# Turning x by 32-bit words on TensorE, each word behind a 512-column matmul, with five block pairs in place of ten

## The chip, the core and the metric

The kernel runs on one core of a Trainium2 chip. A core has five engines that work from queues of their own and wait for each other through counters (semaphores): TensorE (PE in the profile; its weight loads are PEld), VectorE (DVE), ScalarE (ACT), GpSimd (POOL) and SyncE (SP, which here only issues transfers). The metric is the device time of one execution in microseconds. The profile is of one execution; its span is the stretch from its first to its last recorded event.

## What is computed

```python
y = np.matmul(x, weight)                       # x: 16 x 512 x 768, weight: 768 x 768, float32
y = y.reshape(batch, seq, n_heads, head_dim)   # 12 heads of 64
y1, y2 = y[..., :32], y[..., 32:]
out1 = y1 * cos1 - y2 * sin1                   # cos, sin: 512 x 64, halves 1 and 2
out2 = y2 * cos2 + y1 * sin2
out = np.concatenate([out1, out2], axis=-1)    # float32
```

It is a projection of 8192 rows followed by a rotation of each head's two halves.

## The kernel before, in words

The 8192 rows are 64 tiles of 128 rows; four tiles make a group (QB = 4, groups g = 0 to 15). A tile's 768 input columns are six chunks of 128 (CHUNKS: three t, two e). Weights are cast to fp16 once (`w_sb`).

**A tile's way.** SP loads x into one of NX = 10 buffers `xs` (`load`, L210). ACT casts it to fp16 into one of five buffers `xc` (`cast`, L245); the cast orders the columns so that for each t the two values of e lie side by side. TensorE turns it so that input columns lie on partitions (`turn`, L256, or `turn_rows`, L271), into the PSUM pair `pt`. One copy on ACT (L190, the line of the helper that makes all copies) brings it to one of eight buffers `xt`. TensorE multiplies (L337 at both ends of the program, L362 for groups 1 to 14) into six PSUM banks `py`. DVE multiplies the banks by cos and sin (L419, products in `tq` or in the memory of `w_raw`), POOL adds the two halves of the products (L445), and ACT or SP issues the stores (L477).

**Two halves.** From group 1 on each matmul uses one half of the array, rows 0 to 63 (r = 0) or 64 to 127 (r = 1). `walk` (L344) writes each half's list: of every 1536 output columns, banks 0 and 2 in matmuls of 512 columns, bank 1 in matmuls of 256, six chunks each. The second half starts 1024 columns later in the lists (LAG) and takes the banks in another order, so that both halves don't write one bank at once. `both` (L375) merges the two lists by the columns issued so far (`at`). `turn_rows` writes twelve transposes between two calls of `both`: six chunks times two halves, in turn, 64 columns each, the halves into pt0 and pt1. Its copy reads both.

**Blocks.** Ten pairs of tiles (`BLOCKS`, L140: the second half of groups 5 to 13 and of the last) aren't turned by TensorE. Their x is loaded by quarters in such an order (`load_quarter`, L225) that DVE's 32 x 32 stream transpose (`turn_pair`, L299) does the turning: it moves 32-bit words of two fp16 values. Six pairs are loaded by SP as fp32 and cast by ACT (`cast_pair`); four are loaded by POOL, which casts on the way.

**The order.** It is written out in Python: in the main loop (L668 on) each step calls `both` three times, and between these `turns`, `bturns`, `casts`, `pool_loads` and the stores that are due. `do` (L42) adds the waits: an instruction waits for the writers of what it reads and for the readers of what it overwrites; TensorE doesn't wait for itself unless `after` says so. `pump` (L517) issues loads as buffers come free. An fp32 identity (`ident32`) is made by POOL at group 2 in a part of `w_raw`, for an addition at the very end (`add_pe`, L451).

Of the kernel before, what the change touches and what calls it, by code (L numbers as in the profile page):

```python
# [10 lines left out]
FP32 = mybir.dt.float32  # L11
FP16 = mybir.dt.float16
# [4 lines left out]
class Flow:  # L17
# [24 lines left out]
    def do(self, e, make, reads=(), writes=(), dma=None, tick=True, after=0):  # L42
        need = {}
        for k in reads:
            for s, v in self.wrote.get(k, {}).items():
                need[s] = max(need.get(s, 0), v)
        for k in writes:
            for d in (self.wrote, self.readby):
                for s, v in d.get(k, {}).items():
                    need[s] = max(need.get(s, 0), v)  # L50
        if e == "pe":
            need.pop("pe", None)
            if after:
                need["pe"] = after
        waits = self.settle(e, need)
        for s, v in waits[:-1]:
            self.eng[e].wait_ge(self.sem(s), v)  # L57
        i = make(self.eng[e])
        if waits:
            s, v = waits[-1]  # L60
            i.wait_op(self.sem(s), v, "sem-ge")
        name, step = (dma, 16) if dma else (e, 1)
        self.sem(name)
        self.order[name] = len(self.order) + sum(self.count.values())
        at = self.count[name] + step
        if tick or dma:
            i.then_inc(self.sems[name], step)
            self.count[name] = at
            self.known[name, at] = dict(self.seen[e])
        for k in reads:  # L70
            d = self.readby.setdefault(k, {})
            d[name] = max(d.get(name, 0), at)
        for k in writes:
            self.wrote[k] = {name: at}
            self.readby[k] = {}
        return i
# [32 lines left out]
def kernel(  # L109
# [11 lines left out]
    f = Flow(nc, tc)  # L121
    do = f.do
    P = nc.NUM_PARTITIONS

    B, S, H = x.shape
# [5 lines left out]
    NT = H // (2 * P)  # L131
    SB = S // P
    QB = 4
    NG = B * SB // QB
    NTILE = QB * NG
    CHUNKS = [(t, e) for t in range(NT) for e in range(2)]
# [1 line left out]


    BLOCKS = {}  # L140
    for g in range(5, 14):
        BLOCKS[g, 1] = "pool" if g % 2 == 0 and g >= 4 else "sp"
    BLOCKS[LAST, 1] = "sp"

    def sbuf(name, shape, dt):
        return nc.alloc_sbuf_tensor(name, shape, dt).ap()

    NX, NB, NBH, NC, NCP, NXT, NXP, NOV = 10, 3, 3, 5, 2, 8, 4, 4

    ident = sbuf("ident", [P, P], FP16)  # L150
    cold = sbuf("cold", [P, 512], FP16)
    sin_sb = sbuf("sin_sb", [P, SB, D], FP32)
    csn = sbuf("csn", [P, 2, SB, D], FP32)
# [18 lines left out]
        v = mem[:, base : base + 2 * n].rearrange("p (j n) -> p j n", j=2)  # L172
        return v[:, :, lo:hi], sorted(keys)

    ident32 = w_flat[:, 3072 : 3072 + P]
    HOMES0, HOMES, HOMESL = (0, 1024, 3072, 4096), (6144, 0, 3072), (0, 1024, 2048, 3072, 4096, 5120)
    ov_b = [sbuf(f"ov{i}", [P, QB * H], FP32) for i in range(NOV)]
    py = nc.alloc_psum_tensor("py", [P, 6 * 512], FP32).ap()
# [1 line left out]
    pt_b = [pt2[:, i] for i in range(2)]  # L180
# [7 lines left out]
    def copy(e, o, i_):  # L188
        return lambda eng: (
            eng.copy(out=o, in_=i_) if e == "act" else eng.tensor_copy(out=o, in_=i_)  # L190
        )
# [57 lines left out]
    def turn(i, e):  # L249
# [8 lines left out]
        do(e, copy(e, xt_b[z], pt), reads=[f"pt{k}"], writes=[f"xt{z}"])  # L258
        xT[i] = (lambda t, h: xt_b[z][:, t, h, :], f"xt{z}")

    def turn_rows(i, e):

        c = xc[i]
        z = ring("xt", NXT)
        src = xc_b[c].rearrange("p (t m e) -> p t e m", t=NT, e=2)
        pts = [pt_b[r].bitcast(FP16)[:, 0 : H // 2].rearrange(
            "p (t e m) -> p t e m", t=NT, e=2) for r in range(2)]
        for t, h in CHUNKS:
            for r in range(2):
                rows = ts(r, HP)  # L270
                do("pe", lambda eng: eng.transpose(  # L271
                    pts[r][:, t, h, :], src[rows, t, h, :], ident[rows, rows]),
                    reads=[f"xc{c}", "ident"], writes=[f"pt{r}"], tick=(t, h) == CHUNKS[-1])
        do(e, copy(e, xt_b[z].rearrange("p t e (r m) -> p r (t e) m", r=2),
                   pt2.bitcast(FP16)[:, :, 0 : H // 2].rearrange("p r (c m) -> p r c m", m=HP)),
           reads=["pt0", "pt1"], writes=[f"xt{z}"])
        xT[i] = (lambda t, h: xt_b[z][:, t, h, :], f"xt{z}")

    def cast_pair(gh, e="act"):
        k = xs[gh]  # L280
# [40 lines left out]
    def pieces(g, s):  # L321

        out_, lo = [], s * H
        for c0, c1, ps, banks, _ in units(g):
            step = 512 if len(banks) > 1 else c1 - c0
            for k, b in enumerate(banks):
                a, z = max(lo, c0 + k * step), min(lo + H, c0 + (k + 1) * step)
                if a < z:
                    out_.append((a, z, ps[:, a - c0 : z - c0], b))
        return out_  # L330
# [27 lines left out]
    def one(g, i, a, z, r, c, opens, start, ends, whole):  # L358
        s, rows, (t, h), bank = i % QB, ts(r, HP), c, a // 512
        get, key = xT[i]  # L360
        after = closed[g, bank] if not opens and c == CHUNKS[0] else 0
        do("pe", lambda eng: eng.matmul(  # L362
            py[:, a:z], get(t, h)[rows], w_sb[rows, t, h, a - s * H : z - s * H],
            start=start, stop=not opens and ends and whole, skip_group_check=True),
            reads=[key, f"w{t}{h}"], writes=[f"ps{bank}"], tick=ends, after=after)
        if ends and whole and opens:
            closed[g, bank] = f.count["pe"]
        if ends and whole and not opens:
            ready.setdefault(g, set()).add(bank)
# [5 lines left out]
    def both(upto):  # L375

        while True:
            n = [(at[r], r) for r in (0, 1) if lines[r]]
            if not n or min(n)[0] >= upto:
                return  # L380
            r = min(n)[1]
            cols, what = lines[r].pop(0)
            at[r] += cols
            one(*what)
            g = what[0]
            for u in units(g):
                k = g, u[0]
                if k not in roped and {b for b in range(u[0] // 512, u[1] // 512)} <= ready.get(g, set()):
                    roped.add(k)
                    rope(g, u)  # L390
# [76 lines left out]
    def store(g, c0, c1, e):  # L467
# [16 lines left out]
    do("pool", lambda eng: eng.affine_select(  # L484
        out=ident, in_=ident, compare_op=mybir.AluOpType.not_equal, fill=1.0,
        base=0, pattern=[[-1, P]], channel_multiplier=1), writes=["ident"])

    order = [0, 1, "w0", 2, "w1", "w2", 3, "w3", "w4", "w5"]
    for k in order:
# [98 lines left out]
    assert not quarters  # L588
    pump()

    rows_on = [False]
    state = {"cast": 4, "turn": 4, "bturn": 0, "pool": 0}
    pairs = sorted(BLOCKS)
# [14 lines left out]
    def turns(upto, most=NTILE):  # L608
        while state["turn"] < min(upto, NTILE) and most > 0:
            i = state["turn"]  # L610
            state["turn"] += 1
            if not is_block(i):
                most -= 1
                (turn_rows if rows_on[0] else turn)(i, "act")

    def bturns(upto):
        while state["bturn"] < len(pairs):
# [50 lines left out]
    for i in range(QB, NTILE):  # L668
        g, s = divmod(i, QB)
        us = units(g)  # L670
        done_to = (s + 1) * H
        rows_on[0] = QB <= i <= QB * LAST
        if i == QB * (LAST - 2) + 2:
            cast_pair((LAST, 1))
            xb_used[0] += 1
        if i < ROWS:
            if s % 2 == 0:
                for r in range(2):
                    lines[r].extend(walk(i // 2, r))
            for n in range(1, 4):  # L680
                both((i - QB) * 4608 + n * 1536)
                if n == (1 if i > QB else 2):
                    turns(i + T_AHEAD, 1)
        if i == ROWS:
            both(NTILE * 4608)
        for n, p in enumerate(pieces(g, s)) if i >= ROWS else ():
            a, z, _, bank = p
            if n == 1 and i < QB * LAST:
                turns(i + T_AHEAD, 1)
            for c in CHUNKS:  # L690
                mm_piece(i, p, c, c == CHUNKS[0], c == CHUNKS[-1],
                         tick=c == CHUNKS[-1])
            for u in us:
                if u[1] == z:
                    rope(g, u)
        bturns(i + (B_AHEAD if i < QB * (LAST - 2) else 9))
        if i == 2 * QB:
            do("pool", lambda eng: eng.tensor_copy(out=ident32, in_=ident),
               reads=["ident"], writes=["ident32", "wr20"])
        turns(i + 1 + (T_AHEAD if i > QB else 2), 1)  # L700
        casts(i + 1 + (C_AHEAD if i > QB else 4), 1 + i % 2)
        pool_loads(i + P_AHEAD)
        for q in stores.get(i, ()):
            store(*q)
        if g == LAST:
            if s == 2:
                store(g, 0, H, "sp")
            if s == 3:
                store(g, H, 2 * H, "act")
# [44 lines left out]
```

## Time and profile before

| | us |
|---|---|
| median of 3 runs (lowest to highest) | 150.45 (150.42 to 150.75) |
| span of the profiled execution | 148.2 (148.15 unrounded) |
| TensorE busy in it | 140.8 |
| DVE busy | 126.0 |
| POOL busy | 121.8 |
| ACT busy | 79.0 |

The time of a run is some 2.3 us above the profiled span, for what lies around it. The profile's rows of groups give an engine, an operation, its tiles and shapes, the count, the busy time, the mean duration in ns, and the idle time before it with its releaser. A matmul's record lasts longer than its hold on the array, since matmuls are pipelined; how close they follow each other is read from the starts. In the chain and in the timelines a row gives its start and its length.

### The profile page before, as it was taken

To read this page: it belongs to the slowest core of one execution; us is meant where nothing else is said; L and a number is where in the kernel's file an instruction comes from. 1 tells how busy PE (TensorE), PEld (TensorE's weight loads), DVE (VectorE), ACT (ScalarE), POOL (GpSimd) and SP (SyncE) were. 2 spreads that over 40 slices of the span, in tenths; PEclk is the share of its full clock that TensorE was granted. 3 is DMA by queue.
4 is the path that set the end of the run, shared out by engine and by line. 5 is a ranking of instruction groups with operands and counts; after the bars stand their busy time and mean duration, and the time that the engine had idled before them with its cause. 6 is when DMAs were issued, how large, how long until landed. Compare 5 with 4: busy or idle time off the path is not lost.

```text
span 148.2 us, 4422 instructions
## 1 busy us (share of the span) xinstructions
PE 140.8 (95%) x1948; PEld 112.7 (76%) x1948; DVE 126.0 (85%) x99; ACT 79.0 (53%) x94; POOL 121.8 (82%) x73
## 2 busy tenths in 40 slices
PE   6789999999999999999999999999999999999980
PEld 2335578888888888888888888888888888765860
DVE  0335998886988899899989998999989999999991
ACT  3453898777777933557261915375263919931010
POOL 1000396999999998999999999879699999999990
PEclk9999999999999999999999999999999999999999
DMA  3999999999999999999999999999999999998675
GB/s 124 352 395 403 402 406 398 373 379 296 317 366 330 352 353 277 294 408 287 319 355 397 379 323 358 365 408 324 381 365 337 411 409 416 410 408 333 264 297 180
DMA packets 27555, 51.67 MB, mean 349 GB/s; under 512 B 6160, under 2 KB 13072, under 8 KB 27536
## 3 DMA queue, kind: packets, MB, share of 16 engines
q1 hardware_dynamic: 15824, 28.84, 57.0%
q10 hardware_dynamic: 7360, 20.97, 35.9%
q0 software_dynamic: 4352, 1.57, 8.6%
q8 instruction: 15, 0.25, 0.7%
q14 instruction: 4, 0.03, 0.1%
HBM read 27.79 MB, written 25.17 MB: 357 GB/s over the span
## 4 chain that ended last, share of the span: by engine, by line
PE 78%; DVE 12%; DMA 4%; issue 1%; SPq 1%; DVEq 0%
PE py L362 68%; DVE tq L419 8%; PE py L337 5%; PE pt L271 4%; DMA w_raw<-in_weight_dram 4%; DVE w_raw L419 2%; SPq L210 1%; PE pt L256 1%; DVE ov L445 1%; DVE xs L419 1%; SPq L232 1%; DVE w_sb L190 0%; DVEq L57 0%; SPq L749 0%; SPq L119 0%
## 5 line engine op out<-in xcount | busy, mean ns | idle before, releaser
L445 POOL TENSOR_TENSOR ov<-tq 128x512 f32<-128x512 f32 (+3 forms) x35 | 76.8, 2220 | 20.1 <-DVE tq L419 20.1
L362 PE MATMUL py<-w_sb,xt 64*128 64x256 f16 (+1 forms) x864 | 81.5, 323 | 0.0
L419 DVE TENSOR_TENSOR tq<-py,csn 128x1024 f32<-128x1024 f32 (+2 forms) x51 | 74.4, 1496 | 4.6 <-PE py L362 4.5
L362 PEld LDWEIGHTS py<-w_sb,xt 64*128 64x128 f16 x864 | 59.9, 94 | 11.1 <-DVE tq L419 0.4
L190 ACT COPY xt<-pt 128x768 f16<-128x768 f16 x42 | 33.5, 801 | 47.5 <-PE pt L271 46.3
L362 PE MATMUL py<-w_sb,xp 64*128 64x512 f16 (+1 forms) x432 | 42.7, 323 | 0.0
L190 ACT CAST xc<-xs 128x768 f16<-128x768 f32 x44 | 38.8, 911 | 6.9 <-DMA xs<-in_x_dram 6.7
L419 DVE TENSOR_TENSOR w_raw<-py,csn 128x1024 f32<-128x1024 f32 (+1 forms) x22 | 35.3, 1606 | 4.4 <-PE py L362 4.0
L445 POOL TENSOR_TENSOR ov<-w_raw 128x1536 f32<-128x1536 f32 (+2 forms) x15 | 35.4, 2374 | 1.9 <-DVE w_raw L419 1.9
L362 PEld LDWEIGHTS py<-w_sb,xp 64*128 64x128 f16 x432 | 30.7, 94 | 5.0
L337 PE MATMUL py<-w_sb,xt 128*128 128x256 f16 (+1 forms) x102 | 17.0, 317 | 1.4 <-DVE w_sb L190 1.1
L271 PEld LDWEIGHTS pt<-ident,xc 64*128 64x128 f16 x456 | 14.9, 95 | 1.3 <-issue 0.2
L337 PEld LDWEIGHTS py<-w_sb,xt 128*128 128x128 f16 x102 | 9.2, 98 | 7.4 <-DVE w_sb L190 2.7
L271 PE MATMUL pt<-ident,xc 64*128 64x64 f16 x456 | 14.7, 190 | 0.0
L190 ACT CAST xd<-xb 128x1536 f16<-128x1536 f32 x6 | 9.8, 1634 | 0.0
L225 POOL DMA_DIRECT2D xh<-in_x_dram x16 | 9.4, 591 | 0.0
L190 DVE CAST w_sb<-w_raw 128x768 f16<-128x768 f32 x6 | 3.4, 559 | 3.6 <-DMA w_raw<-in_weight_dram 3.6
L299 DVE STREAM_TRANSPOSE xp<-xd 128x768 f32<-128x768 f32 x6 | 5.8, 970 | 0.0
L190 ACT COPY ov<-py 128x256 f32<-128x256 f32 x1 | 0.4, 372 | 10.1 <-POOL ov L445 10.1
L540 PE MATMUL py<-cold 128*128 128x512 f16 x12 | 4.3, 521 | 1.4 <-DVE cold L482 1.4
L190 DVE COPY xt<-pt 128x768 f16<-128x768 f16 x2 | 1.1, 558 | 4.8 <-PE pt L256 4.8
L299 DVE STREAM_TRANSPOSE xp<-xh 128x768 f32<-128x768 f32 x4 | 4.9, 1234 | 0.0
(23 smaller groups left out, 22.6 us busy)
## 6 DMA issues: line engine op xcount, KB each, us to landing
out_dram<-ov ACTq DMA_DIRECT2D x26, 768.0 KB, 9.6
xs<-in_x_dram SPq DMA_DIRECT2D x44, 384.0 KB, 16.4
xb<-in_x_dram SPq DMA_DIRECT2D x24, 192.0 KB, 16.4
out_dram<-ov SPq DMA_DIRECT2D x4, 768.0 KB, 6.2
w_raw<-in_weight_dram SPq DMA_DIRECT2D x6, 384.0 KB, 6.9
xh<-in_x_dram POOLq DMA_DIRECT2D x16, 96.0 KB, 12.1
out_dram<-ov SPq DMA_DIRECT2D x1, 384.0 KB, 2.3
out_dram<-ov ACTq DMA_DIRECT2D x1, 384.0 KB, 2.3
```

Source lines behind the costliest of these rows:

```text
L190: eng.copy(out=o, in_=i_) if e == "act" else eng.tensor_copy(out=o, in_=i_)
L210: do(e, lambda eng: eng.dma_start(out=xs_b[k], in_=x[b].rearrange("(p r) h -> r p h", r=SB)[r]), writes=[f"xs{k}"], dma=f"xs{k}")
L225: do(e, lambda eng: eng.dma_start(out=dst[ts(q, R)], in_=src[r, q]), writes=[f"{name}q{q}"], dma=name)
L232: do(e, lambda eng: eng.dma_start(out=w_raw[:, t, h], in_=wv[t, h]), writes=[f"wr{t}{h}"], dma=f"ov{t}_0" if h else f"xb{t}")
L256: do("pe", lambda eng: eng.transpose(pt[:, t, h, :], src[:, t, h, :], ident), reads=[f"xc{c}", "ident"], writes=[f"pt{k}"], tick=(t, h) == ...
L271: do("pe", lambda eng: eng.transpose(pts[r][:, t, h, :], src[rows, t, h, :], ident[rows, rows]), reads=[f"xc{c}", "ident"], writes=[f"pt{r ...
L299: do("dve", lambda eng: eng.transpose(out=dst, in_=src), reads=rd, writes=[f"xp{z}"])
L337: do("pe", lambda eng: eng.matmul(ps, get(t, h), w_sb[:, t, h, a - s * H : z - s * H], start=start, stop=stop), reads=[key, f"w{t}{h}"], w ...
L362: do("pe", lambda eng: eng.matmul(py[:, a:z], get(t, h)[rows], w_sb[rows, t, h, a - s * H : z - s * H], start=start, stop=not opens and en ...
L419: do("dve", lambda eng: eng.tensor_tensor(out=tq.rearrange("p j (h d) -> p j h d", d=D), in0=ps.rearrange("p (h d) -> p h d", d=D) .unsque ...
L445: do(adder, lambda eng: eng.tensor_tensor(out=ov_b[o][:, ds(c0, w)].rearrange("p (h t d) -> p h t d", t=2, d=HD), in0=tq[:, 0].rearrange(" ...
L540: do("pe", lambda eng: eng.matmul(py[:, ts(b, 512)], cold[:, 0:P], cold, start=True, stop=warmed[0] < WARM - 6), reads=["cold"], writes=[f ...
```

## The change

- `turn_rows` no longer writes its transposes at once. It reads the fp16 tile as fp32 words of two values (three groups of 128 words), makes six transposes of 64 rows x 128 words against an fp32 identity, three in each half, and puts them on a list of that half (`pend`). `both` takes one from the list after each 512-column matmul of the half, and counts 64 columns for it. The copy follows the last of the six; its shape is 2 x 3 x 128 in place of 2 x 6 x 64, as many values.
- `flush` empties the lists where a next tile comes while words are still pending, at group ends and before the last stage.
- Five block pairs stay: the second halves of groups 7, 9, 11, 13 and 15, all loaded by SP. Ten tiles more go through `xs`, the cast and `turn_rows`. POOL issues no loads.
- NX goes from 10 to 12, NBH from 3 to 1. `ident32` has memory of its own and is made at the start.

```diff
-    for g in range(5, 14):
-        BLOCKS[g, 1] = "pool" if g % 2 == 0 and g >= 4 else "sp"
+    for g in range(7, 14, 2):
+        BLOCKS[g, 1] = "sp"
     BLOCKS[LAST, 1] = "sp"
...
-    NX, NB, NBH, NC, NCP, NXT, NXP, NOV = 10, 3, 3, 5, 2, 8, 4, 4
+    NX, NB, NBH, NC, NCP, NXT, NXP, NOV = 12, 3, 1, 5, 2, 8, 4, 4
...
+    pend = [[], []]
+
     def turn_rows(i, e):
...
+        src = xc_b[c].bitcast(FP32).rearrange("p (t m) -> p t m", t=NT)
+        left = [2 * NT]
+
+        def word(r, t):
+            rows = ts(r, HP)
+            dst = pt_b[r][:, t * HP : (t + 1) * HP]
+            do("pe", lambda eng: eng.transpose(dst, src[rows, t, :], ident32[rows, rows]),
+               reads=[f"xc{c}", "ident32"], writes=[f"pt{r}"], tick=t == NT - 1)
+            left[0] -= 1
+            if not left[0]:
+                do(e, copy(e, xt_b[z].rearrange("p t e m -> p (t e m)").rearrange(
+                       "p (t r c) -> p r t c", t=NT, r=2),
+                       pt2.bitcast(FP16)[:, :, 0:H // 2].rearrange("p r (t c) -> p r t c", t=NT)),
+                   reads=["pt0", "pt1"], writes=[f"xt{z}"])
...
+        for r in range(2):
+            pend[r] += [(r, t, word) for t in range(NT)]
...
             one(*what)
+            if cols == 512 and pend[r]:
+                q, t, word = pend[r].pop(0)
+                word(q, t)
+                at[r] += HP
...
+    def flush():
+        while pend[0] or pend[1]:
+            for r in range(2):
+                if pend[r]:
+                    q, t, word = pend[r].pop(0)
+                    word(q, t)
...
-                (turn_rows if rows_on[0] else turn)(i, "act")
+                if rows_on[0]:
+                    flush()
+                    turn_rows(i, "act")
+                    if not lines[0]:
+                        flush()
+                else:
+                    turn(i, "act")
```

## The prediction

> **What bounds the kernel now.** I read the page's busy shares first, then the chain of work that ended last, because a share is only an average, and then the timeline of the stage in which most of the chain lies.
>
> ```profile
> PE 140.8 (95%) x1948; PEld 112.7 (76%) x1948; DVE 126.0 (85%) x99; ACT 79.0 (53%) x94; POOL 121.8 (82%) x73
> ...
> PE 78%; DVE 12%; DMA 4%; issue 1%; SPq 1%; DVEq 0%
> ```
>
> TensorE holds 78% of the chain. DVE holds the end of it (125.9 to 144.9 us), and what it works on there arrives at the pace of TensorE. The chain in order of time (start, length, what) shows how tight TensorE's part is:
>
> ```profile
> 24.99 1.96 PE py L362 x18
> ...
> 33.29 0.20 PE pt L271 x11
> 33.49 1.96 PE py L362 x18
> ...
> 56.34 0.17 PE pt L271 x10
> 56.51 1.93 PE py L362 x19
> ...
> 64.49 0.17 PE pt L271 x10
> 64.66 1.92 PE py L362 x19
> ```
>
> There is no wait in it: matmuls (L362), a turned tile (L271), matmuls. A group that turns four tiles takes 33.49 - 24.99 = 8.50 us, one that turns two takes 64.66 - 56.51 = 8.15. So a turned tile costs 0.35 / 2 = 0.175 us, and the matmuls alone 7.80. Each half of the array (rows 0 to 63, rows 64 to 127) streams 4 tiles x 6 chunks x 768 = 18,432 columns in it, 0.423 ns each: 216 ns for 512 columns, 108 for 256. A turned tile is six transposes in each half: 29 ns each, close to 64 columns at this rate, so their weight loads are hidden. The two halves are two full streams.
>
> **Part 1: words for transposes.** Before, 38 tiles x 0.175 = 6.65 us. After, 48 tiles (ten more, as five block pairs go) with three words in each half. A word is 64 fp32 columns that no row shows. The fp16 transpose above gives 29 ns. The other neighbour is the fp32 matmul at the end (L455; the first line is from the groups kept apart by form):
>
> ```profile
> L271 PE MATMUL pt<-ident,xc 64*128 64x64 f16 x456 | 14.7, 190 | 0.0
> ...
> L455 PE MATMUL py<-tq,w_raw 128*128 128x256 f32 x4 | 1.1, 393 | 0.0
> ...
> L455 PEld LDWEIGHTS py<-tq,w_raw 128*128 128x128 f32 x4 | 0.7, 190 | 0.1
> ```
>
> Its two instructions leave four records, so each takes two passes, 215 ns apart: 0.84 ns a column in a pass, which makes a word 54 ns in one pass and 107 in two. I take 29, from the row with the same operation and size; the ends stay in the range. The sum is then 48 x 3 x 0.029 = 4.2 us, a gain of 2.5; with 54 ns it is 7.8, a loss of 1.1; with 107, 15.4, a loss of 8.8.
>
> The Trainium skill, "TensorE: Matmul & The Clock Gate", section Terms, says that transpose mode is four times faster for fp32. A quarter of the trace's 430 ns for 256 fp32 columns would be 27 ns for a word, an estimate; that speaks for 29, and no run here shows it.
>
> The load of a word's weights, by the L455 row 190 ns against 98 for fp16, some 92 longer, lies behind the 216 ns matmul that the change puts ahead of each. 25 of the 288 words follow another word or a 256-column matmul in their half; they keep up to 0.1 us each, at most 2.5 us. The sum below holds 107 ns from a matmul's start to the start of the word behind it.
>
> **Part 2: a wait that was free.** All words write the same PSUM pair (pt0, pt1), and the one copy on ACT reads both (L190). So the first word of a tile waits for the copy of the tile before; in the order of the changed kernel each of the 48 first words waits on ACT's count. Before, the transposes came in one burst of 0.2 us and the copy had the other 1.9 us of a tile. The timeline (start, length), TensorE and then ACT:
>
> ```profile
> 41.63 0.36 PE L271 MATMUL pt<-ident,xc 64*128 64x64 f16 x11
> 41.80 0.27 PE L362 MATMUL py<-w_sb,xt 64*128 64x256 f16 x1
> 41.83 0.19 PE L271 MATMUL pt<-ident,xc 64*128 64x64 f16 x1
> ```
>
> ```profile
> 42.06 0.80 ACT L190 COPY xt<-pt 128x768 f16<-128x768 f16 x1 [0.52 <-PE pt L271]
> ```
>
> From the start of the last transpose (41.83) to the end of the copy are 1.03 us. TensorE's answer to ACT's count is 0.05 (a cast that ended at 16.20 let a load start at 16.25): 1.1 us in all.
>
> After, the words of a tile are strewn behind 512-column matmuls of their own half. A half has them in runs of twelve, and then twelve of 256 columns (1.30 us) without a place for a word. So a tile's words spread over 0.6 to 1.8 us, and little is left between the last word of one tile and the first of the next. Counted in columns: of 47 such gaps 23 are under 0.05 us, 8 are 0.24 or 0.45, 8 are 0.67 or 0.88, and 8 are 1.09 or more. TensorE takes its queue in order, so everything behind that first word, matmuls of both halves, stands too, for 1.1 minus the gap. The sum of these is 38.5 us if every stall hits the worse half and no gap grows. That is the upper bound.
>
> To get closer I walked the whole order of both kernels: each instruction starts when its engine is free and its counts are reached, with the rows' durations (copy 0.80, cast 0.91, products 2.28 and 1.22, adds 3.47, TensorE as above, one stream per half; ACT's and DVE's neighbours overlap by 0.1 us as in the trace; transfers run at 405 GB/s, from the page's rate by slices). For the kernel before the walk ends DVE's work at 144.8 us, the trace at 144.9. In the changed order, in group 5, a tile's first word is at 58.44, its last at 60.24, and the next tile's first at 61.35 (60.24 + 1.1): 2.91 us a tile, where 8.50 / 4 = 2.12 was enough. The spread of 1.80 is a run of 256s (1.30) and two steps of a 512 and a word (0.49). By groups 1 to 15 the walk adds 2.6, 1.0, 2.9, 3.9, 4.0, 1.2, -0.1, 0.6, 1.8, 1.3, 2.8, 2.0, 1.8, 0.7 and 0.0: **26.5 us**. With the wait taken out, it is 1.9 shorter than before; so the stalls are 28.4.
>
> **Part 3: the rest, at nothing.** Five stream transposes leave DVE (one of 0.97, four of 1.23: 5.9 us), sixteen DMA issues leave POOL (9.4 us): both engines keep up with 8.15 us a group now, with 7.0 and 6.9 us of products and adds, and will have more idle time. ACT gains ten copies and ten casts and loses one cast of a pair (1.63): in groups without a block 4 x (0.91 + 0.80) = 6.8 us, under any group time here; without that cover the copies, and so the stalls, get later. One pair fewer leaves SP's queue in quarters; its loads wait for free buffers (20.1 us on casts), not for bandwidth, and two more buffers let them run further ahead. The fp32 identity, now made by POOL at the start (0.3 us), lies under the weight loads.
>
> **Sum.** 148.2 + 26.5 = 174.7 us of span. Around the span are 150.45 - 148.15 = 2.3 us, the median of three runs against the profiled one: **177.0 us**.
>
> **Rivals.**
> - A word costs one fp32 pass, 54 ns. The walk then adds 30.0: 180.4. For it: L455's columns are as wide. Against: it isn't a transpose. With 107 ns and a load of 213, 38.4: 188.8.
> - Only the half with the waiting word stands. First words alternate between the halves in much of the order, so each loses about half of 28.4: 150.45 - 1.9 + 14.2, about 163. For it: the timeline above has a matmul (41.80) start ahead of the twelfth transpose (41.83), which is earlier in the program; the halves do pass each other by 0.03 us. Against: that was in the array's queue, past all waits.
> - The halves don't pass each other at all. A word stands at the place of the matmul before it, 0.2 us early for the other half, and holds that half back. The walk with starts in order ends 43.3 later: 193.8. Against it is the same pair of lines, 41.80 before 41.83. The Trainium skill, "TensorE: Matmul & The Clock Gate", Part 3, The mechanism, states just this order, start and end strictly in sequence; the trace disagrees by those 0.03 us.
> - The copies fit into the gaps and only the cheaper turn is left: faster, -1.9, **148.5 us**. It is decided where the next tile's first word is issued: the gap must reach 1.1 us. In the new order 39 of 47 don't, but a stall moves the halves against each other, and gaps can grow.
> - The change doesn't take place as said: the words run in bursts, as when the queue of words is emptied at once. In the order 48 tiles have their words one by one or nearly so; 18 of 288 words directly follow another of their half. In bursts each word waits 0.107 us for its load: 48 x 3 x 0.107 = 15.4 in place of 6.65, +8.8: 159.2.
>
> **Chances.** Forecast 0.55; 54 ns a word 0.17; 107 ns 0.04; one half stands 0.08; strict order 0.05; copies fit 0.09; bursts 0.02. The range that leaves out no more than 0.2 goes from the half-stand to the 54 ns case, and each walk may be off by 0.1 us on some 30 stalls: 162 to 184. What the measurement can tell from no change is 0.2%. Faster: 0.09; within 0.2%: 0.02; slower: 0.89.
>
> **What would show it.** In the profile after: ACT's copy starts 0.2 us behind a word and the next word 0.05 behind its end, with TensorE idle or its loads waiting on "ACT xt" tens of times (before: never); groups 3 to 5 near 12 us, group 7 near 8.1; two words of a half 245 ns apart (270 if a word is a pass of 54). DVE and POOL wait more, for TensorE. Wrong would be: no such waits, groups of 8.1 throughout, or words in bursts.

## The result and the profile after

The changed kernel takes **180.78 us** (median of four runs, 180.3 to 181.68), against 150.44 for the kernel before (four runs, 150.18 to 150.75): a ratio of 1.202, 95% interval [1.198, 1.206]. The profiled span grew from 148.2 to 178.5 us, so the whole loss, 30.3 us, lies in the profile. The forecast was 177.0, with 180.4 for the rival in which a word is one fp32 pass. Some executions of a kernel are longer than its others by some per cent, so the times and ratios below are taken from the shorter ones, of the kernel before too.

The page of the changed kernel: busy shares, granted clock, the chain by engine, then the costliest groups around the turn (operation, shapes, count | busy us, mean ns of one | idle time before it and its releaser).

```profile
PE 151.9 (85%) x1780; PEld 115.7 (65%) x1780; DVE 122.2 (68%) x94; ACT 94.4 (53%) x113; POOL 113.0 (63%) x57
...
PEclk9999999999999999999999999999999999999999
...
PE 68%; ACT 14%; DVE 8%; DMA 4%; issue 2%; SPq 1%; DVEq 0%
...
L190 ACT COPY xt<-pt 128x768 f16<-128x768 f16 x52 | 41.4, 798 | 61.9 <-PE pt L273 41.1
L273 PE MATMUL pt<-ident,xc 64*128 64x64 f32 x288 | 54.5, 224 | 18.7 <-ACT xt L190 18.6
L273 PEld LDWEIGHTS pt<-ident,xc 64*128 64x128 f32 x288 | 33.9, 137 | 33.1 <-ACT xt L190 32.2
```

Three things differ from before. ACT is in the chain with 14%, where it had no share at all; its share of busy time, 53%, didn't change, which shows how little that number says. TensorE fell from 95% to 85%. And the words' rows carry idle time that ends with ACT's copy: that is the new wait. The clock isn't part of it: it stays at full speed in every slice.

The waits of the changed kernel (who waited <- for whom: us in total, times, longest):

```profile
POOL ov L458 <- DVE tq L432: 43.2, 20, 14.9
ACT xt L190 <- PE pt L273: 41.1, 30, 4.7
PEld pt L273 <- ACT xt L190: 32.2, 36, 1.2
DVE tq L432 <- PE py L371: 22.3, 20, 2.5
PE pt L273 <- ACT xt L190: 18.6, 31, 0.9
```

Only the third and the last row cost anything, and they are two records of the same stalls (weight loads and matmuls): behind a word that waits, the matmuls of TensorE's queue stand too. DVE and POOL wait more than before because TensorE delivers later, and ACT's own waits are for words that have not been written yet. The third row's 36 waits of at most 1.2 us are the forecast's 1.1 us stalls: by the starts of TensorE's instructions, 33 gaps of 0.40 to 1.23 us that end with a word come to 30.2 us.

One of them, first in the chain of what ended last (start, length, what), then in TensorE's timeline, then in ACT's (in brackets: idle before, and its releaser). "issue" is time in which the engine waited for nothing that the profile shows:

```profile
57.96 1.41 PE py L371 x12
59.37 0.80 ACT xt L190
60.16 0.04 issue
60.21 0.27 PE pt L273
60.48 0.44 PE py L371 x4
60.92 0.01 PE pt L273
60.93 1.35 PE py L371 x12
```

```profile
58.56 0.22 PE L273 MATMUL pt<-ident,xc 64*128 64x64 f32 x1
58.62 0.51 PE L371 MATMUL py<-w_sb,xt 64*128 64x512 f16 x2
58.83 0.22 PE L273 MATMUL pt<-ident,xc 64*128 64x64 f32 x1
58.89 0.46 PE L371 MATMUL py<-w_sb,xt 64*128 64x512 f16 x2
59.10 0.22 PE L273 MATMUL pt<-ident,xc 64*128 64x64 f32 x1
60.21 0.27 PE L273 MATMUL pt<-ident,xc 64*128 64x64 f32 x1 [0.86 <-ACT xt L190]
60.21 0.48 PE L371 MATMUL py<-w_sb,xt 64*128 64x512 f16 x3
```

```profile
59.36 0.80 ACT L190 COPY xt<-pt 128x768 f16<-128x768 f16 x1 [1.59 <-PE py L371]
```

The last word starts at 59.10, the copy 0.26 later, the next tile's first word 0.05 after the copy's end, at 60.21: 1.11 us in which neither half starts anything. Before, the chain at this place read matmuls, turned tile, matmuls, with no other engine. Two words of one half with one 512-column matmul between them (58.56, 58.83) lie 272 ns apart, not the forecast 245: less the matmul's 216, a word is 56 ns.

By groups (last matmul of a group to the next group's last), the loss over groups 1 to 15 is 2.7, 1.3, 3.2, 4.2, 4.4, 1.3, 0.2, 0.7, 2.1, 1.5, 3.1, 2.2, 2.2, 0.9 and 0.0, together some 30 us of the 30.3. Group 7, where the order left the gaps long, runs in 8.4 us, nearly as before (8.15); group 5 takes 12.5 (before 8.15).

### The profile page after: what moved, and what is told of

It reads as the page before. It is cut to its first block, busy times and chain, and to the rows that moved or that the text cites. A ratio compares the mean times of both kernels' runs of the same rounds, so it can differ in the third digit from the quotient of the medians.

```text
span 178.5 us, 4082 instructions
## 1 busy us (share of the span) xinstructions
PE 151.9 (85%) x1780; PEld 115.7 (65%) x1780; DVE 122.2 (68%) x94; ACT 94.4 (53%) x113; POOL 113.0 (63%) x57
## 4 chain that ended last, share of the span: by engine, by line
PE 68%; ACT 14%; DVE 8%; DMA 4%; issue 2%; SPq 1%; DVEq 0%
PE py L371 57%; ACT xt L190 14%; PE pt L273 7%; DVE tq L432 5%; DMA w_raw<-in_weight_dram 4%; PE py L346 4%; DVE w_raw L432 2%; SPq L210 1%; PE pt L256 1%; DVE xs L432 0%; SPq L232 0%; DVE ov L458 0%; DVE w_sb L190 0%; DVEq L57 0%; SPq L775 0%
## 5 line engine op out<-in xcount | busy, mean ns | idle before, releaser
L371 PE MATMUL py<-w_sb,xt 64*128 64x256 f16 (+1 forms) x1104 | 107.2, 323 | 0.0
L371 PEld LDWEIGHTS py<-w_sb,xt 64*128 64x128 f16 x1104 | 75.8, 95 | 9.9 <-DVE tq L432 0.4
L190 ACT COPY xt<-pt 128x768 f16<-128x768 f16 x52 | 41.4, 798 | 61.9 <-PE pt L273 41.1
L273 PE MATMUL pt<-ident,xc 64*128 64x64 f32 x288 | 54.5, 224 | 18.7 <-ACT xt L190 18.6
L273 PEld LDWEIGHTS pt<-ident,xc 64*128 64x128 f32 x288 | 33.9, 137 | 33.1 <-ACT xt L190 32.2
L190 ACT CAST xc<-xs 128x768 f16<-128x768 f32 x54 | 47.6, 907 | 7.4 <-DMA xs<-in_x_dram 7.3
L371 PE MATMUL py<-w_sb,xp 64*128 64x512 f16 (+1 forms) x192 | 21.3, 323 | 0.0
L371 PEld LDWEIGHTS py<-w_sb,xp 64*128 64x128 f16 x192 | 13.9, 96 | 1.2
L190 ACT COPY ov<-py 128x256 f32<-128x256 f32 x1 | 0.4, 372 | 10.1 <-PE py L468 10.1
L256 PEld LDWEIGHTS pt<-ident,xc 128*128 128x128 f16 x36 | 2.1, 98 | 2.6 <-ACT xc L190 1.8
L256 PE MATMUL pt<-ident,xc 128*128 128x128 f16 x36 | 3.0, 220 | 0.8 <-ACT xc L190 0.8
```

Source lines behind the costliest of these rows:

```text
L256: do("pe", lambda eng: eng.transpose(pt[:, t, h, :], src[:, t, h, :], ident), reads=[f"xc{c}", "ident"], writes=[f"pt{k}"], tick=(t, h) == ...
L273: do("pe", lambda eng: eng.transpose(dst, src[rows, t, :], ident32[rows, rows]), reads=[f"xc{c}", "ident32"], writes=[f"pt{r}"], tick=t == ...
L371: do("pe", lambda eng: eng.matmul(py[:, a:z], get(t, h)[rows], w_sb[rows, t, h, a - s * H : z - s * H], start=start, stop=not opens and en ...
```

## The experiments

The theory: a word in the strewn order is early for the copy of the tile before, TensorE's queue stands, and that is the whole loss apart from the words' own columns. The rivals: the words themselves cost it, the five pairs that go cost it, or the 512-column places.

**1. Nothing waits for the copy.** The copy reads the fp16 tile instead of the PSUM pair.

```diff
-                       pt2.bitcast(FP16)[:, :, 0:H // 2].rearrange("p r (t c) -> p r t c", t=NT)),
-                   reads=["pt0", "pt1"], writes=[f"xt{z}"])
+                       xc_b[c].rearrange("p (r t c) -> p r t c", r=2, t=NT)),
+                   reads=[f"xc{c}"], writes=[f"xt{z}"])
```

> ACT's copy reads the fp16 tile in SBUF in place of the words in PSUM, so nothing reads the turned words and no word has to wait for a copy; the matmuls then multiply tiles that were not turned. All else of the changed kernel stays: 288 words, their places, the copies' count and size. Wait theory: the 28 us of stalls go, and what is left is 48 tiles x 3 words x 0.056 us = 8.1 in place of 6.65 in the kernel before: 152.0 us. Word theory (the words or their weight loads cost the time themselves): stays near 180. Block theory (ten more tiles through loads, casts and copies cost it): stays near 180 too.

Measured: 153.75 us (153.21 to 154.69), 1.019 [1.008, 1.030] of before. The words, their places, the copies and the five pairs are all still there (only that nothing reads the words any more), and 27.0 us of the 30.3 are gone: the wait is the cause. No wait of TensorE for the copy is left in its profile, and its groups 2 to 13 take 8.2 to 8.5 us. The time is 1.8 us above the expectation. In the profile 7.0 us lie behind the start of the last fp16 matmul (5.5 before), and ACT's casts wait 26.5 us for x loads (7.3 in the changed kernel); what delays these wasn't settled.

**2. The words at once.** Emptying the lists directly behind each tile brings back the bursts of before.

```diff
                     turn_rows(i, "act")
-                    if not lines[0]:
-                        flush()
+                    flush()
```

> Each tile's six words are issued at once, as the transposes of the kernel before were; nothing else of the changed kernel moves. Wait theory: the copy has the rest of the tile's time again, no stalls; a word behind a word of its half takes 62 ns by the bursts in the trace of the changed kernel (25.205, 25.261, 25.323), so about 0.19 us a tile: 152.4 us. Word theory: weight loads are no longer hidden, so it gets slower than 180.8.

Measured: 152.46 us (151.89 to 153.23), 1.014 [1.010, 1.018]. TensorE's and ACT's timeline of this kernel:

```profile
41.47 0.36 PE L273 MATMUL pt<-ident,xc 64*128 64x64 f32 x6
41.65 1.68 PE L371 MATMUL py<-w_sb,xt 64*128 64x256 f16 x18
```

```profile
41.88 0.80 ACT L190 COPY xt<-pt 128x768 f16<-128x768 f16 x1 [0.52 <-PE pt L273]
```

All six words start within 0.18 us, the copy runs beside 1.68 us of matmuls, and it is done (42.68) long before the next tile's words are due (43.60). The same 288 words with the same wait cost next to nothing where they stand together; it is their places in TensorE's queue that make the wait dear.

**3. Five pairs with the transposes of before.** The kernel before with `BLOCKS`, NX and NBH of the change.

```diff
-    for g in range(5, 14):
-        BLOCKS[g, 1] = "pool" if g % 2 == 0 and g >= 4 else "sp"
+    for g in range(7, 14, 2):
+        BLOCKS[g, 1] = "sp"
...
-    NX, NB, NBH, NC, NCP, NXT, NXP, NOV = 10, 3, 3, 5, 2, 8, 4, 4
+    NX, NB, NBH, NC, NCP, NXT, NXP, NOV = 12, 3, 1, 5, 2, 8, 4, 4
```

> The kernel before with its fp16 transposes in bursts, but five block pairs, none by POOL, and twelve x buffers. Wait theory: ten more turned tiles x 0.175 us on TensorE and no stall: 150.45 + 1.75 = 152.2 us. Block theory: the ten tiles make most of the loss, 170 or more.

Measured: 151.91 us (151.75 to 152.39), 1.009 [1.006, 1.012]. Ten more turned tiles at 0.175 us are 1.75; 1.5 was found (the kernel before beside it: 150.40). Nothing else of that part of the change costs or gains anything that can be seen. Beside run 2, on the same chip, it also compares the two ways of turning: 152.46 - 151.91 = 0.55 us for 48 tiles, against the words, though the lowest and highest runs of the two overlap.

**4. A word behind any matmul.** If the 1.30 us runs of 256-column matmuls without a place spread a tile's words, places there should end most stalls.

```diff
-            if cols == 512 and pend[r]:
+            if pend[r]:
```

> A word follows any matmul of its half, 256 columns too, not only those of 512. Wait theory: the words of a tile lie within some 0.7 us, so the gap before the next tile's first word is over 1.1 us in nearly all places: 153.1 us by the same walk through the order as for the prediction. Word theory: a weight load behind a 256-column matmul is hidden less well, so not faster than 180.8.

Measured: 153.43 us (152.89 to 153.99), 1.016 [1.007, 1.025]: one condition is worth 27.4 of the 30.3 us. So it isn't interleaving in itself, but the spread. The words of one tile start from 44.74 to 45.29 in this kernel's timeline, those of the tile before from 42.73 to 43.56; the copy between them (43.82 to 44.62) fits into the gap of 1.18 us, by a tenth.

**5. Half the copy.** One copy per half, 384 values, so that a half's first word waits for a copy half as long.

```diff
             left[0] -= 1
+            if t == NT - 1:
+                do(e, copy(e, xt_b[z].rearrange("p t e m -> p (t e m)").rearrange(
+                       "p (t r c) -> p r t c", t=NT, r=2)[:, r],
+                       pt_b[r].bitcast(FP16)[:, 0:H // 2].rearrange("p (t c) -> p t c", t=NT)),
+                   reads=[f"pt{r}"], writes=[f"xt{z}h{r}"])
             if not left[0]:
-                do(e, copy(e, xt_b[z].rearrange("p t e m -> p (t e m)").rearrange(
-                       "p (t r c) -> p r t c", t=NT, r=2),
-                       pt2.bitcast(FP16)[:, :, 0:H // 2].rearrange("p r (t c) -> p r t c", t=NT)),
-                   reads=["pt0", "pt1"], writes=[f"xt{z}"])
...
```

> Each half's three words have a copy of their own (384 values, an estimated 0.48 us from 0.80 for 768 and 0.37 for 256), so the next tile's words of a half wait for that half alone. Words, places and block pairs are those of the changed kernel. Wait theory: the wait is shorter but a half's words still lie between 512-column matmuls and its gaps are short: by the walk 169.0 us, less than half of the stalls gone. Rival (the whole stall is one of the two halves waiting for the other's words, which go late): near 155.

Measured: 169.07 us (168.63 to 169.37), 1.1265 [1.125, 1.128]: 11.7 of the 30.3 us go. The group of half copies, and the wait that is left:

```profile
L190 ACT COPY xt<-pt 128x384 f16<-128x384 f16 x96 | 44.6, 480 | 43.7 <-PE pt L273 32.3 <-PE py L372 9.2
```

```profile
PEld pt L273 <- ACT xt L190: 19.9, 33, 1.3
```

A copy of half the size takes 0.48 and not 0.40 us, and the wait falls from 32.2 to 19.9 us (12.3), about what the time shows. The edit does two things at once, a shorter copy and a wait for one half's words alone, so it doesn't say how much each gives; but a loss that changes with the copy is a loss through the copy.

**6. The words with ten pairs.** `BLOCKS`, NX and NBH as before, the strewn words as in the change.

```diff
-    for g in range(7, 14, 2):
-        BLOCKS[g, 1] = "sp"
+    for g in range(5, 14):
+        BLOCKS[g, 1] = "pool" if g % 2 == 0 and g >= 4 else "sp"
...
-    NX, NB, NBH, NC, NCP, NXT, NXP, NOV = 12, 3, 1, 5, 2, 8, 4, 4
+    NX, NB, NBH, NC, NCP, NXT, NXP, NOV = 10, 3, 3, 5, 2, 8, 4, 4
```

> The words behind 512-column matmuls, with the ten block pairs and ten x buffers of the kernel before: 38 tiles of words in place of 48, and in the block groups two in a group. Wait theory: the walk gives 167.0 us, 13 less than the changed kernel for ten tiles, since a block pair widens the gaps of its whole group. Rival (a fixed price for each turned tile): 30.3 x 38 / 48 = 24 us, so 174.5.

Measured: 167.16 us (166.91 to 167.71), 1.115 [1.113, 1.117]. With 38 tiles instead of 48 the wait is 19.3 us, 22 times (32.2, 36 times with five pairs). Groups 5 to 13 turn two tiles each and have more room: groups 5 to 7 take 9.1 to 9.2 us and groups 8 to 11 8.1 to 8.4 (before 8.15), where the changed kernel takes 8.4 to 12.5. So the two parts of the change are not independent: the five pairs alone cost 1.5 us (run 3), in company with the strewn words 180.78 - 167.16 = 13.6.

**7. Bursts of words with ten pairs.** Run 2's edit and run 6's: only the kind of the transposes is changed against before. Beside the ten pairs of run 6:

```diff
-                    if not lines[0]:
-                        flush()
+                    flush()
```

> Words in a burst, with the ten block pairs and ten x buffers of the kernel before: the turn alone is exchanged, six words for twelve fp16 transposes. A word in a burst takes 62 ns by the trace of the changed kernel, two fp16 transposes 58: 38 x (0.19 - 0.175) = 0.6 us at most: 150.4 to 151.0 us, hardly to be told from the kernel before. If the loads of fp32 words hold the array 107 ns each: 154.0.

Measured: 150.37 us (150.25 to 151.16) against 150.13 for the kernel before beside it: 1.0023 [1.0007, 1.0040]. Its chain has the form of before:

```profile
25.26 0.21 PE pt L273 x6
25.46 1.95 PE py L371 x18
27.42 0.18 PE pt L273 x6
27.60 1.92 PE py L371 x18
```

A tile is turned in 0.18 to 0.21 us, as with twelve fp16 transposes (0.17 to 0.20): three words of a half, 56 to 62 ns apart, are no shorter than six fp16 transposes at 29. There was no cheaper turn to be had.

**8. Behind any matmul, with ten pairs**, the combination that should have come closest to the kernel before (runs 4 and 6 together). Beside the ten pairs of run 6:

```diff
-            if cols == 512 and pend[r]:
+            if pend[r]:
```

> Words behind any matmul of their half, with the ten block pairs and ten x buffers of the kernel before. Wait theory: no stalls, 38 x 3 x 0.056 = 6.4 us in place of 6.65 on TensorE, but a few gaps at the start still short: 151.4 us by the walk. If words were the better turn, it would be under 150.0.

Measured: 156.00 us (154.01 to 156.18), 1.036 [1.030, 1.041]: the expectation fell. The profile is of a run of 160.06 us, with a span of 158.3: 10.1 more than before. Of these 6.7 are lost in group 13, which takes 15.1 us (8.4 before), and 3.4 in groups 1, 3 and 4. ACT's timeline in group 13, and the weight load of the word that waits:

```profile
118.10 0.91 ACT L190 CAST xc<-xs 128x768 f16<-128x768 f32 x1
122.46 0.92 ACT L190 CAST xc<-xs 128x768 f16<-128x768 f32 x1 [3.44 <-DMA xs<-in_x_dram]
...
125.47 0.88 ACT L190 CAST xc<-xs 128x768 f16<-128x768 f32 x1 [2.09 <-DMA xs<-in_x_dram]
...
126.25 1.56 ACT L190 CAST xd<-xb 128x1536 f16<-128x1536 f32 x1
...
127.72 0.78 ACT L190 COPY xt<-pt 128x768 f16<-128x768 f16 x1
```

```profile
128.55 0.18 PEld L273 LDWEIGHTS pt<-ident,xc 64*128 64x128 f32 x1 [4.20 <-ACT xt L190]
```

It is the same wait with another length: the copy stands in ACT's queue behind casts, and these wait for x. Where the words are strewn, the copy comes later in ACT's order than the next casts; in a burst it comes ahead of them. By stretches (us, busy time and instructions of PE, PEld, DVE, ACT and POOL, granted clock, DMA share, GB/s):

```profile
118.00:126.00 8.00, 6.69 (x86) 5.32 (x81) 7.57 (x6) 2.46 (x4) 8.00 (x6) 1.00 1.03 408
126.00:134.00 8.00, 5.45 (x45) 4.53 (x47) 3.43 (x3) 4.87 (x6) 4.13 (x4) 0.57 0.94 374
```

The transfers are at 408 GB/s. From 110 to 130 us the DMA queue that carries the stores takes 70.8% of the engines, that of the loads 32.2%, and a load of x lands 14.3 us after its issue (median; 8.9 over the whole changed kernel). That alone doesn't explain the delay: in run 7, which loses nothing, it is 17.0 in the same stretch.

TensorE starts nothing from 124.37 to 128.55, and in the middle of this its granted clock falls to half, from 126.9 to 133.7. The 5.15 us of it that lie behind the stall add up to 2.6 us to the loss. The Trainium skill, "TensorE: Matmul & The Clock Gate", Part 1, has a rule for this: after an idle window of some 3.4 us the clock falls to half. The traces agree only in part: the changed kernel's 36 stalls of at most 1.2 us left the clock at 1.0 throughout, but here it fell 2.5 us after the last matmul's start, when TensorE had been busy for 1.23 of the last 3.41 us, so no wholly idle window was needed.

**9. The same with NX 12** (NBH 2), in case buffers made x late. Against run 8:

```diff
-    NX, NB, NBH, NC, NCP, NXT, NXP, NOV = 10, 3, 3, 5, 2, 8, 4, 4
+    NX, NB, NBH, NC, NCP, NXT, NXP, NOV = 12, 3, 2, 5, 2, 8, 4, 4
```

> The run before last (words behind any matmul, ten block pairs) with twelve x buffers in place of ten. Its miss (158.1 for 151.4) went with ACT waiting 18.2 us for x loads in 10 places, and with copies that stand behind these casts in ACT's queue, so that TensorE waited up to 4.2 us for a copy. If too few loads in flight are the cause: the waits go and the time is 151.4 to 152. If it is the loads' rate against the stores near the end, two more buffers change little: 154 or more, varying from run to run.

Measured: 156.69 us (two runs, 156.14 and 157.24), 1.043 [1.034, 1.051]: two more buffers don't help; it isn't for want of buffers. The profile, of the run of 156.14 us, shows the same wait in group 13, which takes 13.3 us: a cast that waits for x, the copy behind the casts, the longest wait of a word's load (3.3 us), and the clock in slices (in tenths; it is half from 125.8 to 129.2):

```profile
121.75 0.90 ACT L190 CAST xc<-xs 128x768 f16<-128x768 f32 x1 [2.07 <-DMA xs<-in_x_dram]
...
124.55 0.81 ACT L190 COPY xt<-pt 128x768 f16<-128x768 f16 x1
```

```profile
PEld pt L273 <- ACT xt L190: 6.3, 7, 3.3
```

```profile
PEclk9999999999999999999999999999999987999998
```

**10. The same with casts a tile later** (`C_AHEAD` 4 in place of 5), so that fewer of them stand ahead of a copy. Against run 8:

```diff
-    C_AHEAD, T_AHEAD, B_AHEAD, P_AHEAD = 5, 3, 4, 20
+    C_AHEAD, T_AHEAD, B_AHEAD, P_AHEAD = 4, 3, 4, 20
```

> The run of words behind any matmul with ten block pairs (158.1 us, ten x buffers), with the casts one tile later in the program (C_AHEAD 4 in place of 5), so that fewer copies stand behind a cast that waits for its x load. If copies behind late casts made the 7 us of that run's miss: 151 to 153. If late loads stop TensorE in whatever order ACT works: still 156 or more.

Measured: 157.17 us (155.78 to 157.88), 1.043 [1.033, 1.052], a miss too. In the profile, of a run of 160.05 us, a copy still stands behind a late cast, now that of a block pair:

```profile
126.75 1.54 ACT L190 CAST xd<-xb 128x1536 f16<-128x1536 f32 x1 [5.70 <-DMA xb<-in_x_dram]
...
128.20 0.79 ACT L190 COPY xt<-pt 128x768 f16<-128x768 f16 x1
```

That a late load reaches TensorE through ACT's queue is seen three times. Why x is late in group 13 of these kernels, and not with bursts and ten pairs (run 7) or any matmul and five (run 4), stays open.

**11. One pair more in the kernel before** (eleven), the other direction of the change's second part.

```diff
-    for g in range(5, 14):
+    for g in range(4, 14):
```

> The kernel before, with an eleventh block pair (second half of group 4, loaded by POOL): the opposite of what the change did. If a block pair is worth the TensorE time of two turned tiles where DVE has room (7.0 + 1.2 us of 8.5 in that group): 2 x 0.175 = 0.35 us less, 150.1 by the median of the kernel before. If POOL's loads or DVE's transpose reach the path: the same or slower.

Measured: 150.09 us (149.29 to 150.84) against 149.97 beside it, 0.9998 [0.997, 1.003]: not to be told from no change. No version was found that beats the kernel before.

A second PSUM target for the words, which would take away the wait itself, wasn't tried; the program has one, the pair `pt`, beside the six banks of `py`.

## Why the prediction was right, point by point

- **The wait (part 2): right.** The loop of 1.1 us, put together from three rows of before, measured 1.11 (0.26, 0.80 and 0.05). The walk's pattern by groups is the measured one, from 4.4 us in group 5 (walk: 4.0) to 0.2 in group 7 (walk: -0.1). Runs 1, 2 and 4 each take away the wait in another manner; 2.1 to 3.4 us are left above the kernel before beside them (150.40).
- **The word (part 1): the term that was mis-sized.** The prediction chose 29 ns, from the fp16 transpose of the same size; measured are 56, which is close to one pass of the fp32 matmul in row L455 (54). That is 48 x 3 x 0.027 = 3.9 us on TensorE; the walk with 54 made it 3.5, and 180.4 in place of 177.0, which is 0.4 from the measured time. So it was the condition of the first rival, with a chance of 0.17, that came true; the forecast was 3.8 us too low, about what this term was short. That L455 "isn't a transpose" was the wrong reason to leave a row of the same type for one of the same operation. By the Trainium skill, "TensorE: Matmul & The Clock Gate", Terms, which the prediction named (transpose mode four times faster for fp32, an estimate of 27 ns), the sum would have been that of the forecast; the trace disagrees with its 56.
- **So the gain was none.** "With the wait taken out, it is 1.9 shorter than before" and the rival's 148.5 rest on the 29 ns. At 56 the turn costs 8.1 us in place of 6.65, and the kernels without the wait are all slower than before (1.009 to 1.019 with five pairs).
- **The load of a word: too dear in the bound.** The prediction took a load of 190 ns from the L455 row and 107 a word in bursts, 159.2 us. The words' own load record is 137 ns (fp16: 95), bursts run at 62 ns a word, and run 2 took 152.46. Behind a 512-column matmul the load is hidden, as said (272 - 216 = 56 ns a word); the first word after a stall has a record of 0.27 us in place of 0.22, which fits a load that nothing hides.
- **The halves.** Neither "one half stands" (163) nor "strict order" (193.8) held. In the stall no matmul of either half starts for 1.11 us; and had a word's place held back the other half, the time by the walk would have been 13 us longer than it is.
- **The rest at nothing (part 3): right in the changed kernel.** Run 3 finds 1.5 us for the five pairs, no more than their turned tiles cost TensorE (1.75). DVE and POOL wait more, at no cost. The cover named there, that ACT keeps up and x comes in time, wears thin only with less slack: runs 8 to 10 show what it costs when a late cast stands ahead of a copy. The 2.3 us around the span were 1.9 in the profiled run (180.38 - 178.5).

## What to carry to other kernels

Small work strewn between large matmuls is hidden only if nobody waits for it as a whole: with one target, count from its last piece through the engine that empties it to its next first piece, and compare that with the gap the order leaves. If the gap is shorter, the queue stands for the difference each time (here 33 times, 30 us); put the pieces together, so that the emptying has the rest of the period. Where a new operation has no row, let the row of the same data type bound it as well as the row of the same operation, and test the gain against the worse of the two.

## What the runs showed of the chip that was not expected

- A transpose of 64 rows x 128 fp32 words holds its half for 56 ns, about twice the 29 of the fp16 transpose of the same size: two values in the time of two. Words save instructions, but no time.
- A copy of half the values from PSUM took 0.48 us on ACT, against 0.80 for the whole: by an estimate from these two, some 0.16 us of it don't shrink (2 x 0.48 - 0.80).
- 33 stalls of at most 1.23 us left the granted clock at full. A stall of 4.2 us (run 8) halved it for 6.8 us, beginning 2.5 us after the last matmul's start; one of 3.3 us (run 9) halved it for 3.4 us, beginning 0.4 us after the stall's end.
